# Last gate, third and fourth chunk: low parts by an accumulating DMA instead of VectorE's subtraction

## The chip, the cores and the metric

The kernel runs on one core of one Trainium2 chip. What counts is the device time of one execution in microseconds; a run's number is the median of several executions. The kernel before the change takes 1843.85 us (three runs, 1843.67 to 1844.14).

The engines are called by their names in the profile: PE (TensorE matmuls), PEld (TensorE's weight loads, which overlap the matmuls), DVE (VectorE), ACT (ScalarE), POOL (GpSimd) and SP (SyncE, which issues nearly all DMAs). L118 is line 118 of the kernel; a line can be a helper's.

## What is computed

The reference is a decoder of two layers on 512 tokens of width 2048, in float32. Layer 0 mixes by sparse attention, layer 1 by stick-breaking attention. After its mixer each layer does the same:

```
x = layer_norm(ALPHA * x + h, ln_g[i], ln_b[i])
x = x + (p[i] @ w_ple[i]) * sigmoid(x @ w_ple_gate[i])
```

The change is in the last product of the program, `x @ w_ple_gate[1]`: a 512 x 2048 array times a 2048 x 2048 matrix, followed by a sigmoid, a product and a sum. It is called the last gate here.

## The kernel before

Activations are held transposed: sixteen blocks of 128 features by 512 tokens. A product is a loop over the sixteen blocks of 128 weight rows, the k-blocks, which adds into PSUM banks of 128 output features by 512 tokens.

**Three matmuls for one.** TensorE takes its operands in a shorter form (fp32r). To keep float32 accuracy each operand is split: the high part is the number rounded to that form, the low part is what is left, number minus high part. `mm3` (L144 to L147) issues three matmuls for each product of two such pairs: high with high (L145), high weights with low activations (L146), low weights with high activations (L147). So the low weights `wl` are first needed by the third matmul of a k-block.

**How a weight block gets there.** SP loads raw weights, two k-blocks in one DMA, into one of three `raw` buffers (`next_raw`, L225). `plain_items` takes each k-block of it through `split` (L140): ScalarE copies `raw` into `wh` (which rounds it), and VectorE subtracts `wh` from `raw` into `wl`. Both come from rings of three buffers (`weight_parts`). A profile row shows L118 for every operation that ScalarE and VectorE issue, because a recording helper issues them there; the tiles' names tell them apart.

**The order of the work.** TensorE's order is the order of the program text. ScalarE, VectorE, SP and GpSimd get theirs from a scheduler that simulates the program when it is built, apart from the pieces that are pinned. Within an engine the instructions then run strictly in that order. `Ahead` is an iterator over weight blocks: it holds `n` blocks that are written down in the program ahead of the matmuls that use them, two by default, and so says how far ahead the text of the program asks for a block. How far ahead it can really be made is set by the buffers.

**The last gate.** Its 2048 output features are done in chunks of 512, 512, 512, 256, 128 and 128 (`LAST_PARTS`). The first two run interleaved, in eight banks. The third and the fourth run one after the other, each over sixteen k-blocks, with four banks and with two: twelve and six matmuls for a k-block. While a chunk runs, the pieces of the chunk before are put between its matmuls: `gated` (ScalarE's sigmoid out of the bank into `sg`, VectorE's product with `E` and its sum onto `f`) and `store` (a DMA from SP to the output, L1311). The two chunks of 128 have their weights loaded eight k-blocks to a DMA (L206) and copied four k-blocks at a time.

Of the kernel before, what the change touches and what calls it, by code (L numbers as in the profile page):

```python
# [11 lines left out]
F32R = mybir.dt.float32r  # L12
I32 = mybir.dt.int32
AF = mybir.ActivationFunctionType
ALU = mybir.AluOpType
# [6 lines left out]
NK = D // 128  # L22
# [24 lines left out]
def run(gen):  # L47
    for _ in gen:
        pass


def steps(gen, n):
    for _ in range(n):
        next(gen, None)
# [23 lines left out]
def trunk_kernel(  # L78
# [16 lines left out]
    nc = tc.nc  # L95
# [31 lines left out]
    act, dve, pool = (Paced(e) for e in (nc.scalar, nc.vector, nc.gpsimd))  # L127
# [9 lines left out]
    def bank(i, name="ps"):  # L137
        return psum.tile([128, 512], F32, name=name, tag=f"bank{i}")

    def split(hi, lo, src, eng=dve):  # L140
        act.activation(hi, src, AF.Copy)
        eng.tensor_tensor(lo, src, hi.bitcast(F32), ALU.subtract)
# [16 lines left out]
    def fblock(n):  # L159
        return F[n // 4][:, n % 4]  # L160
# [12 lines left out]
    units = []  # L173
# [10 lines left out]
    raws = deque()  # L184
    halves = []
    sent = [0]
# [5 lines left out]
    def next_raw():  # L192
        while sent[0] < len(units) and len(raws) < (6 if homes and sent[0] in kv_units else 3):
            housed[0] += 1
            if homes and sent[0] in kv_units and housed[0] % 2:
                raw = homes[housed[0] // 2 % 3]
            else:
                raw = top.tile([128, 2, 512], F32, name="raw", tag="raw", bufs=3)
            unit = units[sent[0]]
            if len(unit) == 1:  # L200
                _, k, n = unit[0].shape
            else:
                k, n = 2, unit[-1]
            raw = raw.rearrange("p a n -> p (a n)")[:, : k * n].rearrange("p (k n) -> p k n", k=k)
            if len(unit) == 1:
                nc.sync.dma_start(raw, unit[0])  # L206
            else:
                src, a, b, c0, n = unit
                rows = src.rearrange("(k p) n -> p k n", p=128)
                step = b - a  # L210
                if sent[0] < 2:

                    for i, cut in enumerate(((0, H if sent[0] else NSEL, T), (0, T))):
                        for lo, hi in zip(cut, cut[1:]):
                            halves.append((raw[:, i, lo:hi], rows[:, a + i * step, c0 + lo : c0 + hi]))
                    if len(halves) == 6:
                        for n in (1, 3, 4, 2, 5, 0):
                            nc.sync.dma_start(*halves[n])
                elif isinstance(c0, tuple):

                    for half, out in enumerate(raw.rearrange("p k (h n) -> h p k n", h=2)):
                        at = D // 2 * half + c0[0]
                        nc.sync.dma_start(out, rows[:, a : b + 1 : step, at : at + n // 2])
                else:
                    nc.sync.dma_start(raw, rows[:, a : b + 1 : step, c0 : c0 + n])  # L225
            raws.append(raw)
            sent[0] += 1
        return raws.popleft()
# [41 lines left out]
    def weight_parts():  # L270
        return tuple(top.tile([128, 512], F32R, name=n, tag=n, bufs=3) for n in ("wh", "wl"))

    def plain_items(jobs):
        for n, nk in jobs:
            if n <= 128:
                for k in range(0, nk, 4):
                    if k % 8 == 0:
                        raw = next_raw()
                    parts = weight_parts()
                    four = [w[:, : 4 * n].rearrange("p (k n) -> p k n", k=4) for w in parts]  # L280
                    split(*four, raw[:, k % 8 : k % 8 + 4])
                    yield from zip(*([w[:, a] for a in range(4)] for w in four))
                continue
            for _ in range(nk // 2):
                raw = next_raw()
                for a in range(2):
                    wh, wl = weight_parts()
                    split(wh[:, :n], wl[:, :n], raw[:, a])
                    yield wh, wl
# [36 lines left out]

    def plain_stream(*jobs):
        return Ahead(plain_items(jobs), 2)

    def gemm_w(items, get, banks, n=512, order=range(NK)):  # L330

        for i, kb in enumerate(order):
            wh, wl = next(items)
            x = get(kb)
            for j, out in enumerate(banks):
                a, b = j * 128, min(n, (j + 1) * 128)
                mm3(out[: b - a], (wh[:, a:b], wl[:, a:b]), x, i == 0, i == len(order) - 1)
                yield
# [62 lines left out]
    def pumped(gen, every=1):  # L401

        for i, _ in enumerate(gen):
            if bg and i % every == 0:
                one()
            yield

    def drain():
        while bg:
            one()  # L410
# [290 lines left out]
    for k in (4, 5, 6, None, 7, None, 0, 1, 2, 3):  # L701
        if k is None:
            first = 4 * (units[-1][1] == 14)
# [338 lines left out]
    def finish_layer(layer, resid, last, keep, early, ahead):  # L1042
# [112 lines left out]
        for c in SEVENS:  # L1155
            M = product_banks(3 - c)
            gemm = pumped(gemm_s(wo, four, M), 9 if c == 1 else 7)
            if c == 2:
                steps(gemm, 35)
                parts = weight_parts()  # L1160
# [49 lines left out]
        raw = next_raw()  # L1210
# [44 lines left out]
        fourth = embed(3, (2, 3, 4, 5))  # L1255
        steps(fourth, 4)
        parts = LAST_PARTS if layer else PARTS
        gitems = plain_stream(*[(n, NK) for n in parts]).prime()

        def scaled(n):  # L1260
            dve.tensor_tensor(fblock(n), fblock(n), rs, ALU.mult)
# [31 lines left out]
        with tc.tile_pool(name=f"pe{layer}", bufs=1, side="right") as ep:  # L1293

            places = deque((S, rs))
            if not layer:
                kv_room.append([[ep.tile([128, T], F32R, name=f"e{x}{n}") for x in "hl"] for n in range(2)])

            def gated(n, b, t=slice(0, T)):
                if layer:  # L1300
                    sg = ep.tile([128, T], F32, name="sg", tag="sg", bufs=4)[:, t]
                else:
                    places.rotate(1)
                    sg = places[0]
                act.activation(sg, b[:, t], AF.Sigmoid)
                dve.tensor_tensor(sg, sg, E[n][:, t], ALU.mult)
                dve.tensor_tensor(fblock(n)[:, t], fblock(n)[:, t], sg, ALU.add)

            def store(n, k, t=slice(0, T)):
                rows = last[n * 128 : (n + k) * 128, t].rearrange("(j p) t -> p j t", p=128)  # L1310
                nc.sync.dma_start(rows, F[n // 4][:, n % 4 : n % 4 + k, t])  # L1311

            def close(n, b):
                for t in (slice(0, H), slice(H, T)):
                    gated(n, b, t)
                    store(n, 1, t)

            banks = two[0]
            plan = list(zip(parts[1:], ((2, 3, 4, 5), (6, 7, 0, 1), (4, 5), (2, 3)))) + [(0, ())]
            if layer:  # L1320
                plan[3:] = [(128, (0,)), (128, (1,)), (0, ())]
            for c, (n, where) in enumerate(plan):
                part = BLOCKS[layer][c]
                for j, b in enumerate(banks):
                    if len(banks) == 1:
                        bg.append(lambda n=part[j], b=b: close(n, b))
                        continue
                    bg.append(lambda n=part[j], b=b: gated(n, b))
                    if j % 2 and part[j - 1] + 1 == part[j]:
                        bg.append(lambda n=part[j - 1]: store(n, 2))  # L1330
                    elif j % 2:
                        bg.extend(lambda n=n: store(n, 1) for n in part)
                bg.extend(early.get(c, ()))
                if not n:
                    break
                if c:
                    banks = [bank(b, "g") for b in where]
                    order = range(NK) if layer or c < 3 else PAIRS
                    gemm = gemm_close(gitems, banks[0]) if where == (1,) else gemm_w(gitems, plain, banks, n, order)
                else:  # L1340
                    banks = two[1]
                gemm = pumped(gemm, 4 if n == 512 else 2)
                if c == 3:
                    steps(gemm, 14 if layer else 6)
                    ahead(gemm)
                run(gemm)
                drain()
            drain()
# [41 lines left out]

    pk_, pv_ = ExitStack(), ExitStack()
    finish_layer(0, xT, x2, (pk_, pv_), first_sums, first_blocks)


# [174 lines left out]
    class Sticks:  # L1569
# [3 lines left out]
        units = [(3, 3), (1, 1), (3, 2), (1, 0), (3, 1), (2, 2), (3, 0), (2, 1), (0, 0), (2, 0)]  # L1573
# [211 lines left out]
    with ExitStack() as keep:  # L1785
        finish_layer(1, x2, outT, (keep, keep), lambda E8: {}, lambda gemm: None)
# [53 lines left out]
```

## Time and profile before

| | |
|---|---|
| median of three runs | 1843.85 us |
| the profiled execution, its span | 1842.2 us |
| PE busy | 1835.4 us, 9568 matmuls |
| VectorE busy in the whole run | 1377.9 us |
| ScalarE busy in the whole run | 989.8 us |
| GpSimd busy in the whole run | 4.7 us, 20 instructions |
| third chunk of the last gate | 1750.1 to 1793.6 us |
| fourth chunk | 1793.6 to 1815.4 us |
| last matmul starts | 1837.09 us |

The profile gives the profiled execution's span, from its first to its last instruction, and no other time for it; the difference to the median of the runs is 1.65 us. Its page has busy times per engine, the chain of work that ended last, and groups of equal instructions; the views used here beside the page are the waits of an engine, the windows (busy time of each engine in a stretch), the timeline of single instructions, and the groups in a stretch by form. In a group's row the number before the bar is the count; behind it stand the busy time in us, the mean duration in ns, and the engine's idle time before these instructions with what ended it. A matmul's row in the timeline shows 0.39 us, while the next starts 0.23 us later: they are pipelined.

### The profile page before, as it was taken

Reading aid. Unit: us, or ns where it says so; the run is one execution under the profiler, and the core shown is the slowest. Engines: PE = TensorE matmul, PEld = TensorE weight load, DVE = VectorE, ACT = ScalarE, POOL = GpSimd, SP = SyncE. Lnnn points to the kernel's source line nnn. Section 1 sums busy time; section 2 is a strip of 40 time slices with the busy share of each in tenths; the row PEclk is TensorE's granted clock in tenths of the full one; section 3 lists DMA queues with packets and bytes.
Section 4 is the critical chain, followed back from the end, with each engine's and each line's share of the span. In section 5 each row is a group of like instructions: output and inputs, shape, how many; then the busy total and the mean of one; then the engine's idle time right before and its main releaser. Section 6 shows DMA issues by size and latency. Waiting matters only on the chain.

```text
span 1842.2 us, 26158 instructions
## 1 busy us (share of the span) xinstructions
PE 1835.4 (100%) x9568; PEld 1580.4 (86%) x9568; DVE 1377.9 (75%) x2721; ACT 989.8 (54%) x1801; POOL 4.7 (0%) x20
## 2 busy tenths in 40 slices
PE   9999999999999999999999999999999999999998
PEld 8898888888888899888888899998888889988887
DVE  5668678575556789976568998888878789987434
ACT  3546333455555544575346544468888754557322
POOL 0000000000000000000000000000000000000000
PEclk9999999999999999999999999999999999999999
DMA  6442333322222344333437633323122245343333
GB/s 199 125 121 69 92 94 101 92 69 69 69 59 69 107 123 114 125 116 103 138 110 236 198 101 100 104 91 92 58 69 80 66 118 149 109 123 101 115 102 115
DMA packets 118000, 197.68 MB, mean 107 GB/s; under 512 B 9200, under 2 KB 37872, under 8 KB 117872
## 3 DMA queue, kind: packets, MB, share of 16 engines
q1 hardware_dynamic: 117872, 196.02, 35.9%
q8 instruction: 75, 1.23, 0.3%
q14 instruction: 53, 0.43, 0.1%
HBM read 187.60 MB, written 8.39 MB: 106 GB/s over the span
## 4 chain that ended last, share of the span: by engine, by line
PE 99%; DMA 0%; DVE 0%; ACT 0%; SPq 0%; issue 0%; ACTq 0%
PE g L145 13%; PE g L147 13%; PE g L146 13%; PE m L147 7%; PE m L145 7%; PE m L146 7%; PE o L146 4%; PE o L145 4%; PE o L147 4%; PE q L146 3%; PE q L147 3%; PE q L145 3%; PE iq L147 1%; PE iq L146 1%; PE iq L145 1%; PE z L1639 1%
## 5 line engine op out<-in xcount | busy, mean ns | idle before, releaser
L118 ACT ACTIVATE wh<-raw 128x512 fp32r<-128x512 f32 (+2 forms) x597 | 336.7, 565 | 537.9 <-PE g L146 211.2
L118 DVE TENSOR_TENSOR wl<-raw,wh 128x512 fp32r<-128x512 f32 (+2 forms) x596 | 361.5, 607 | 272.1 <-ACT wh L118 256.6
L145 PE MATMUL g<-xh,wh 128*128 128x512 f32 x1023 | 403.1, 394 | 0.0
L147 PE MATMUL g<-xh,wl 128*128 128x512 f32 x1023 | 399.0, 390 | 0.0
L146 PE MATMUL g<-xl,wh 128*128 128x512 f32 x1023 | 398.9, 390 | 0.0
L147 PEld LDWEIGHTS g<-xh,wl 128*128 128x128 f32 x1023 | 192.0, 188 | 40.7
L146 PEld LDWEIGHTS g<-xl,wh 128*128 128x128 f32 x1023 | 192.3, 188 | 37.2
L145 PEld LDWEIGHTS g<-xh,wh 128*128 128x128 f32 x1023 | 192.2, 188 | 37.1
L146 PE MATMUL o<-xl,wh 128*128 128x512 f32 x256 | 99.7, 390 | 0.0
L145 PE MATMUL o<-xh,wh 128*128 128x512 f32 x256 | 99.6, 389 | 0.0
L147 PE MATMUL o<-xh,wl 128*128 128x512 f32 x256 | 99.6, 389 | 0.0
L145 PE MATMUL q<-xh,wh 128*128 128x512 f32 x256 | 99.6, 389 | 0.0
L146 PE MATMUL q<-xl,wh 128*128 128x512 f32 x256 | 99.6, 389 | 0.0
L147 PE MATMUL q<-xh,wl 128*128 128x512 f32 x256 | 99.6, 389 | 0.0
L147 PE MATMUL m<-c,sl 128*128 128x256 f32 x320 | 90.9, 284 | 0.0
L145 PE MATMUL m<-c,sh 128*128 128x256 f32 x320 | 90.7, 283 | 0.0
L146 PE MATMUL m<-c,sh 128*128 128x256 f32 x320 | 90.5, 283 | 0.0
L118 ACT ACTIVATE sh<-f 128x512 fp32r<-128x512 f32 x77 | 48.0, 624 | 67.6 <-DVE f L118 64.8
L147 PE MATMUL m<-xh,wl 128*128 128x256 f32 x256 | 72.6, 284 | 0.0
L145 PE MATMUL m<-xh,wh 128*128 128x256 f32 x256 | 72.5, 283 | 0.0
L146 PE MATMUL m<-xl,wh 128*128 128x256 f32 x256 | 72.4, 283 | 0.0
L118 ACT ACTIVATE sh<-st 128x512 fp32r<-128x512 f32 x70 | 43.6, 624 | 52.2 <-DVE st L118 51.5
(378 smaller groups left out, 4061.0 us busy)
## 6 DMA issues: line engine op xcount, KB each, us to landing
raw<-w_in_a SPq DMA_DIRECT2D x95, 512.0 KB, 3.7
raw<-w_in_b SPq DMA_DIRECT2D x64, 512.0 KB, 3.7
raw<-w_ple_gate SPq DMA_DIRECT2D x44, 512.0 KB, 3.9
raw<-w_o_a SPq DMA_DIRECT2D x24, 512.0 KB, 4.5
raw<-w_o_b SPq DMA_DIRECT2D x24, 512.0 KB, 4.5
f<-w_kv_b SPq DMA_DIRECT2D x16, 512.0 KB, 4.6
raw<-w_kv_b SPq DMA_DIRECT2D x16, 512.0 KB, 4.3
raw<-w_ple_gate SPq DMA_DIRECT2D x24, 256.0 KB, 2.9
```

Of the source, the lines that this page charges most:

```text
L118: ins = method(*args, **kw)
L145: pe.matmul(out, a[0], b[0], start=start, stop=False)
L146: pe.matmul(out, a[0], b[1], start=False, stop=False)
L147: pe.matmul(out, a[1], b[0], start=False, stop=stop)
L1639: pe.matmul(z, down if kb % 2 else tri, p, start=False, stop=n == 1, skip_group_check=True)
```

## The change

In the last gate of layer 1, for the third chunk (512 features) and the fourth (256), the low part is no longer made by VectorE. For each of the 32 k-blocks

- ScalarE copies `raw` with the factor -1 into `wm`, which leaves the negated high part there;
- GpSimd issues a DMA (L341 of the changed kernel) that reads the same raw weights from HBM once more and adds them onto `wm`, which leaves raw minus high part, the low part;
- ScalarE copies `raw` into `wn`, the high part, as before into `wh`.

`wn` and `wm` are new rings of six buffers each, in a pool that exists during the last gate only. While these 32 blocks are asked for, `Ahead` is set to hold five blocks instead of two. `first` is the index of the weights' place in the list of loads.

```
+    def summed_items(pool_, parts):
+        first = sent[0] - len(raws)
+        for n in parts:
+            for _ in range(NK // 2):
+                src, a, b, c0, n = units[first]
+                first += 1
+                raw = next_raw()
+                for i, row in enumerate((a, b)):
+                    wh = pool_[0].tile([128, 512], F32R, name="wn", tag="wn", bufs=6)[:, :n]
+                    wl = pool_[0].tile([128, 512], F32R, name="wm", tag="wm", bufs=6)[:, :n]
+                    act.activation(wl, raw[:, i], AF.Copy, scale=-1.0)
+                    nc.gpsimd.dma_start(wl, src[row * 128 : row * 128 + 128, c0 : c0 + n], accum_op=ALU.add)
+                    act.activation(wh, raw[:, i], AF.Copy)
+                    yield wh, wl
...
-        gitems = plain_stream(*[(n, NK) for n in parts]).prime()
+        tail_pool = []
+
+        def tail_items():
+            jobs = [(n, NK) for n in parts]
+            yield from plain_items(jobs[:2])
+            gitems.n = 5
+            yield from summed_items(tail_pool, parts[2:4])
+            gitems.n = 2
+            yield from plain_items(jobs[4:])
+
+        gitems = Ahead(tail_items(), 2) if layer else plain_stream(*[(n, NK) for n in parts])
+        gitems.prime()
...
         with tc.tile_pool(name=f"pe{layer}", bufs=1, side="right") as ep:
...
+            tail_pool.append(ep)
```

TensorE's order does not move; only the names of its weight tiles change. GpSimd's program, which ended with the masks of layer 1's attention, gets the DMAs as its last work. Before:

```order
20 L1563 AFFINE_SELECT wk<-wk 128x128
21 L1567 AFFINE_SELECT gone_12011<-gone_12011 128x128
22 L1567 AFFINE_SELECT gone_12012<-gone_12012 128x128
23 L1836 UNCONDITIONAL_BRANCH
24 L1836 ISA
```

and now:

```order
20 L1590 AFFINE_SELECT wk<-wk 128x128
21 L1594 AFFINE_SELECT gone_12011<-gone_12011 128x128
22 L1594 AFFINE_SELECT gone_12012<-gone_12012 128x128
23 L341 DMA wm<-w_ple_gate 128x512 x16
24 L341 DMA wm<-w_ple_gate 128x256 x16
25 L1863 UNCONDITIONAL_BRANCH
26 L1863 ISA
```

All 32 DMAs stand there in the order of the blocks, with nothing between them.

On ScalarE, at the end of the fourth chunk (`wh` 128x512 are the copies for the two closing chunks, `sg` the sigmoids of the fourth), the order before was

```order
1373 L118 ACTIVATE sg<-g 128x512
1374 L118 ACTIVATE wh<-raw 128x256 x9
1375 L118 ACTIVATE wh<-raw 128x512 x2
1376 L118 ACTIVATE sg<-g 128x512
1377 L118 ACTIVATE wh<-raw 128x512
```

and is now

```order
1425 L118 ACTIVATE wn<-raw 128x256
1426 L118 ACTIVATE wm<-raw 128x256
1427 L118 ACTIVATE wn<-raw 128x256
1428 L118 ACTIVATE wm<-raw 128x256
1429 L118 ACTIVATE wh<-raw 128x512 x2
1430 L118 ACTIVATE wn<-raw 128x256
1431 L118 ACTIVATE wm<-raw 128x256
1432 L118 ACTIVATE wh<-raw 128x512
1433 L118 ACTIVATE sg<-g 128x512 x2
```

Each block has two copies there in place of one, the one into `wn` first, and two copies for the fifth chunk have moved ahead of the last block's pair. On VectorE the 32 subtractions are gone, and the products and sums of `gated` stand without them in between.

## The prediction

> **What bounds the kernel now.** I read the page's busy shares and chain first, then TensorE's waits over the whole run, and then the windows of the three stretches that the change can reach.
>
> ```profile
> PE 1835.4 (100%) x9568; PEld 1580.4 (86%) x9568; DVE 1377.9 (75%) x2721; ACT 989.8 (54%) x1801; POOL 4.7 (0%) x20
> ...
> PE 99%; DMA 0%; DVE 0%; ACT 0%; SPq 0%; issue 0%; ACTq 0%
> ...
> PE spun L167 <- DVE xl L118: 1.4, 1, 1.4
> PE z L145 <- DVE t L116: 0.3, 1, 0.3
> ```
>
> TensorE (PE) is the bound from end to end: 99% of the chain is its matmuls, and in the whole run it waited for another engine twice, 1.7 us together, both far from the last gate. The subtractions that the change removes are never what TensorE waits for. The windows below are the third chunk, the fourth chunk, and the two closing chunks; columns are length, busy time of PE, PEld, DVE, ACT and POOL, granted clock, share of the DMA engines and GB/s.
>
> ```profile
> 1750.10:1793.60 43.50, 43.50 (x193) 36.02 (x193) 15.72 (x24) 11.62 (x20) 0.00 (x0) 1.00 0.33 106
> 1793.60:1815.40 21.80, 21.80 (x97) 18.04 (x97) 12.16 (x24) 9.53 (x21) 0.00 (x0) 1.00 0.56 172
> 1815.40:1837.30 21.90, 21.90 (x100) 18.12 (x98) 8.16 (x14) 4.85 (x10) 0.00 (x0) 1.00 0.19 62
> 975.00:985.00 10.00, 10.00 (x46) 8.28 (x45) 6.69 (x14) 6.12 (x13) 0.00 (x0) 1.00 0.87 271
> ```
>
> PE is busy for all of each stretch, at a granted clock of 1.00, while VectorE (DVE) is busy 15.72 of 43.50 us and 12.16 of 21.80 us. So a lighter VectorE has nothing to give here: the best case is no change, and the question is whether the new supply line keeps pace.
>
> **The pace that the supply must keep.** TensorE takes one block of 128 weight rows (wh and wl) after the other. A row of the timeline has start, length, engine, line, operation and tiles.
>
> ```profile
> 1744.67 0.63 ACT L118 ACTIVATE wh<-raw 128x512 fp32r<-128x512 f32 x1 [2.09 <-PE g L146]
> ...
> 1747.39 0.63 ACT L118 ACTIVATE wh<-raw 128x512 fp32r<-128x512 f32 x1 [2.09 <-PE g L146]
> ...
> 1790.48 0.39 PE L146 MATMUL g<-xl,wh 128*128 128x512 f32 x1
> ...
> 1790.71 0.39 PE L147 MATMUL g<-xh,wl 128*128 128x512 f32 x1
> ...
> 1790.91 0.42 ACT L118 ACTIVATE wh<-raw 128x256 fp32r<-128x256 f32 x1 [2.30 <-PE g L146]
> 1790.94 0.39 PE L145 MATMUL g<-xh,wh 128*128 128x512 f32 x1
> ...
> 1791.17 0.19 PEld L147 LDWEIGHTS g<-xh,wl 128*128 128x128 f32 x1
> ...
> 1793.63 0.42 ACT L118 ACTIVATE wh<-raw 128x256 fp32r<-128x256 f32 x1 [2.30 <-PE g L146]
> ...
> 1793.95 0.58 ACT L118 ACTIVATE sg<-g 128x512 f32<-128x512 f32 x1
> ...
> 1803.15 0.42 ACT L118 ACTIVATE wh<-raw 128x256 fp32r<-128x256 f32 x1 [0.94 <-PE g L146]
> ...
> 1804.51 0.42 ACT L118 ACTIVATE wh<-raw 128x256 fp32r<-128x256 f32 x1 [0.94 <-PE g L146]
> ```
>
> ScalarE (ACT) refills a buffer whenever TensorE frees one, so its steps show TensorE's: 1747.39 - 1744.67 = 2.72 us for a block in the third chunk, 1804.51 - 1803.15 = 1.36 us in the fourth. 16 blocks each make 43.5 and 21.8 us, the windows above.
>
> In the change, wm (the new wl) has six buffers. Block k may be written when TensorE has done with block k-6, and is needed when block k's first L147 loads its weights. From that come two allowances for "GpSimd's time for one DMA, S, plus its landing after that, Ld". In the fourth chunk: ScalarE starts 0.04 us after the releasing matmul ends (1790.48 + 0.39 to 1790.91), writes wn, 0.32 us later (1793.63 to 1793.95) wm for 0.42 us, so wm stands about 0.8 us after the block's end. It is needed five blocks and 0.25 us later (1790.94 to 1791.17): 5 x 1.36 + 0.25 - 0.8 = 6.25 us. In the third chunk, with 0.63 us instead of 0.42, it is 5 x 2.72 + 0.25 - 1.15 = 12.7 us. These are allowances for delay; for rate, S must stay under 2.72 and 1.36 us.
>
> **The change part by part.** Removed: 32 subtractions on VectorE, 16 of each width.
>
> ```profile
> L118 DVE TENSOR_TENSOR wl<-raw,wh 128x512 fp32r<-128x512 f32 x16 | 11.1, 693 | 24.9 <-ACT wh L118 24.2 <-PE g L146 0.7
> L118 ACT ACTIVATE wh<-raw 128x512 fp32r<-128x512 f32 x17 | 10.7, 632 | 29.0 <-PE g L146 28.2 <-DVE wl L118 0.7
> L118 DVE TENSOR_TENSOR wl<-raw,wh 128x256 fp32r<-128x256 f32 x16 | 6.8, 424 | 13.5 <-ACT wh L118 13.5
> L118 ACT ACTIVATE wh<-raw 128x256 fp32r<-128x256 f32 x16 | 6.7, 418 | 17.0 <-PE g L146 17.0
> ```
>
> That is 11.1 + 6.8 = 17.9 us of VectorE, all of it under matmuls: worth 0. A gain is excluded because PE had no wait there.
>
> Added on ScalarE: 32 negated copies, priced as the plain copies of those rows, 16 x 0.632 + 16 x 0.418 = 16.8 us. ScalarE goes to about 11.6 + 10.1 = 21.7 of 43.5 us and 9.5 + 6.7 = 16.2 of 21.8 us: it fits, cost 0.
>
> Added on GpSimd: 32 DMAs, which read the weights a second time: 16 x 256 KB and 16 x 128 KB, or 4.2 and 2.1 MB, some 96 GB/s in either chunk. No DMA of GpSimd and none that accumulates is in the trace, so S and Ld are bounded by SP's plain ones (KB each, median us from issue to landing; then the duration of the issue in ns).
>
> ```profile
> raw<-w_ple_gate SPq DMA_DIRECT2D x44, 512.0 KB, 3.9
> ...
> raw<-w_ple_gate SPq DMA_DIRECT2D x24, 256.0 KB, 2.9
> ...
> raw<-w_ple_gate SPq DMA_DIRECT2D x32, 128.0 KB, 2.5
> ...
> L225 SPq DMA_DIRECT2D raw<-w_ple_gate x13: 367/368/368, 1748.8 to 1804.1; - x13
> ```
>
> S from below: SP's issue, 0.37 us. S from above: one DMA at a time, the whole landing, 2.5 us for 128 KB and 2.9 for 256 KB. Ld from below 2.5 us; from above twice that, 5.0, because the sum reads two operands.
>
> In the third chunk both ends pass: S is at most 2.9 against 2.72, short by 0.2 us over the ten blocks that the six buffers don't cover, 2 us against an allowance of 12.7. In the fourth chunk eleven DMAs (blocks 5 to 15) have to be issued after it has begun; the first can start at 0.8 us, the last must have landed at 15 x 1.36 + 0.25 = 20.65 us. Where S is over 1.36, TensorE is therefore late by 0.8 + 11 S + Ld - 20.65 = **11 S + Ld - 19.85 us**. Lower ends: below nothing, so 0. Upper ends: 11 x 2.5 + 5.0 - 19.85 = 12.7 us. I take the lower end, since SP's issue is the nearest row (the same two-dimensional DMA from the same tensor) and the formula stays at nothing up to S = 1.58 us at Ld = 2.5, over four times that row.
>
> The page "DMA: Bandwidth & Descriptors" of the Trainium skill (section on the anatomy of one DMA on the gpsimd path) states about 2.0 us plus bytes over 436e3 for such a DMA; an estimate by it is 2.3 us for 128 KB, inside the 6.25 us, and no run here shows it.
>
> DMA traffic: the fourth chunk goes from 172 to some 268 GB/s, and with the second operand more engine time than that; 271 GB/s at a share of 0.87 were reached before (the last window row above) without a PE wait. 0, with Ld's upper end standing for crowding.
>
> Moved: two copies for the fifth chunk now stand on ScalarE ahead of block 15's pair. Their raw load starts when block 11 has been copied, at 6 x 1.36 + 0.8 = 9.0 us, and lands at 12.9 (3.9, row above); wm 14 stands at 13.0, the two copies end near 14.2, and wm 15 near 15.0. That leaves 5.65 us of the allowance for S + Ld, and 2.9 are used at my value. SP has no other wait added; GpSimd has nothing else queued.
>
> After the last gate nothing changes:
>
> ```profile
> 1837.09 0.28 PE L366 MATMUL g<-xh,wl 128*128 128x256 f32 x1
> 1837.41 0.66 ACT L118 ACTIVATE sg<-g 128x256 f32<-128x256 f32 x2 [7.78 <-PE g L366]
> ```
>
> **Sum.** The profiled execution spans 1842.2 us, 1.65 below the median of the runs, 1843.85, which covers what lies around the span. Removed 0, ScalarE 0, DMAs 0, moved 0; I add 0.3 for a partly exceeded allowance: 1844.2 us.
>
> **Rivals.** First, and on the slower side: GpSimd's own time per DMA sets the rate. Place: L341's 128x256 DMAs in the fourth chunk. It decides from S = 1.58 us, and over the 3.7 us that make 0.2% from S = 1.91. For it: a path that this kernel never used, and a second operand to describe. Against it: the 0.37 us row. At S = 2.5, Ld = 2.5: 27.5 + 2.5 - 19.85 = 10.2 us, so 1854.0; at S = 1.91 1847.6.
>
> Second: the sums land late, S + Ld over 6.25 us, with the DMA engines crowded. Every round of six buffers then pays the excess; at 10 us two rounds, 2 x 3.75 = 7.5 us, 1851.4. Against it: the slowest row above needs 3.9 us at 512 KB.
>
> Third: VectorE holds GpSimd off while it works. In the fourth chunk it still has 4 pairs for the third chunk's gates:
>
> ```profile
> L118 DVE TENSOR_TENSOR f<-f,sg x8: 683/692/693, 1752.1 to 1801.3; 128x512 f32<-128x512 f32 x8
> ...
> L118 DVE TENSOR_TENSOR sg<-sg,e x4: 683/690/695, 1794.6 to 1800.3; 128x512 f32<-128x512 f32 x4
> ```
>
> If each shut GpSimd out for its 0.69 us, 8 x 0.69 = 5.5 us are lost; at S = 1.36 that makes 0.8 + 15.0 + 5.5 + 2.5 - 20.65 = 3.1 us, 1847.0. The page "SBUF — State Buffer" of the Trainium skill (section "SBUF: two separate sides") warns of such a trap, VectorE keeping GpSimd from writing descriptors during a two-port operation. By its section "Who interferes with whom" tensor_tensor has no such mode and contends only with GpSimd's reads, which speaks for a small chance; this trace can't show either.
>
> Fourth: faster, 1843.0 or below. It would need PE to lose the 0.23 us step between matmuls, for which no row speaks.
>
> **How the numbers follow.** Forecast, no wait or one under 3.7 us: 0.55, at 1844.2, own range 1843.4 to 1847.5. GpSimd's rate 0.28, late landing 0.11, VectorE's hold 0.03 (it stays within 0.2%), faster 0.03. A measurement of this kernel can't tell less than about 0.2%, 3.7 us, from no change. So faster 0.03, same 0.55 + 0.03 = 0.58, slower 0.28 + 0.11 = 0.39. The range runs from 1843.0 to 1858, the upper ends of S and Ld (12.7 us) and 1.5 us more; what lies above is S over 2.5.
>
> **What would show it.** Right: PE's waits name neither wm nor DMA in the last 92 us, the fourth chunk stays at 21.8 us, and GpSimd's DMAs stand at under 1.4 us each. Wrong: PE L147 waits for wm in the fourth chunk. If the waits grow from block to block and GpSimd's DMAs follow each other without a gap, it is the first rival; if GpSimd has gaps and issue to landing is over 6 us, the second; if its DMAs are long only beside VectorE's pairs, the third. A wait already in the third chunk would mean S over 2.72 us, above my bound.

## The result and the profile after

The changed kernel takes 1853.83 us (1852.69 to 1855.94), the kernel before 1843.85: a ratio of 1.0056, 95% interval 1.0038 to 1.0074. It is slower by 10 us, or 0.56%, and the interval lies clear of 1. In a later comparison it took 1852.70 us (1850.68 to 1854.73) against 1843.63, a ratio of 1.0050 (1.0037 to 1.0063). The profiled execution of it spans 1854.2 us, 1.74 us less than its own time of 1855.94; before spanned 1842.2. So the traces have 12.0 us to explain.

First the page of the changed kernel (busy times, the queue that GpSimd feeds, the chain), then TensorE's waits over the whole run.

```profile
PE 1841.1 (99%) x9568; PEld 1583.6 (85%) x9568; DVE 1360.9 (73%) x2689; ACT 1002.3 (54%) x1833; POOL 32.4 (2%) x52
...
q0 software_dynamic: 4608, 6.29, 2.1%
...
PE 94%; issue 3%; POOL 1%; DMA 1%; ACT 0%; DVE 0%; SPq 0%; POOLq 0%; ACTq 0%
```

```profile
PE g L147 <- DMA wm<-w_ple_gate: 4.3, 3, 3.8
PE g L145 <- ACT wh L118: 2.1, 1, 2.1
```

VectorE lost its 32 subtractions (17.0 us of busy time), ScalarE gained 32 copies (12.5 us), GpSimd 32 DMAs. TensorE, which waited nowhere in the last gate before, now has one long wait for a sum (`wm`), two short ones, and one long wait for an ordinary copy (`wh`), which the change did not touch. But the waits make only 6.4 of the 12.0 us. The rest is in TensorE's own timeline, here at the end of the second chunk and at the end of the fourth:

```profile
1746.80 0.39 PE L147 MATMUL g<-xh,wl 128*128 128x512 f32 x1
1749.32 0.50 PE L145 MATMUL g<-xh,wh 128*128 128x512 f32 x1 [2.13 <-ACT wh L118]
...
1752.07 0.63 PE L147 MATMUL g<-xh,wl 128*128 128x512 f32 x1
1752.50 0.63 PE L145 MATMUL g<-xh,wh 128*128 128x512 f32 x1
...
1753.78 0.63 PE L145 MATMUL g<-xh,wn 128*128 128x512 f32 x1
...
1819.62 0.39 PE L146 MATMUL g<-xl,wn 128*128 128x512 f32 x1
1823.80 0.79 PE L147 MATMUL g<-xh,wm 128*128 128x512 f32 x1 [3.79 <-DMA wm<-w_ple_gate]
1824.39 0.63 PE L145 MATMUL g<-xh,wn 128*128 128x512 f32 x1
...
1829.08 0.55 PE L147 MATMUL g<-xh,wl 128*128 128x512 f32 x1
```

Behind each hole the matmuls start 0.43 us apart for a while (from 1751.22 to 1754.21, and eleven steps from 1824.39 to 1829.08) instead of 0.227. The windows of the same execution (columns as in the prediction) show it as a granted clock of 0.83 and 0.68:

```profile
1740.00:1750.00 10.00, 7.87 (x34) 5.93 (x32) 3.87 (x6) 4.19 (x9) 1.73 (x2) 1.00 0.82 215
1750.00:1760.00 10.00, 10.00 (x38) 8.03 (x38) 2.77 (x4) 3.92 (x8) 2.59 (x3) 0.83 0.95 236
1760.00:1797.60 37.60, 37.60 (x168) 31.14 (x167) 2.77 (x4) 14.51 (x30) 12.08 (x14) 1.00 0.80 179
1797.60:1820.00 22.40, 21.88 (x93) 16.85 (x91) 7.41 (x11) 11.58 (x29) 9.52 (x11) 1.00 0.87 199
1820.00:1827.00 7.00, 3.21 (x9) 2.53 (x9) 1.71 (x3) 1.19 (x2) 0.00 (x0) 0.68 0.59 151
```

In the order of time, counted from one matmul's start to the next, less the usual step: the hole before 1749.32 costs 1749.32 - 1746.80 - 0.23 = 2.3 us; the slow matmuls behind it 2.0 (15 steps in 5.40 us instead of 3.40); the hole before 1823.80 costs 1823.80 - 1819.62 - 0.23 = 3.95; the slow ones behind it 2.7 (13 steps in 5.66 instead of 2.95). That is 10.95 us. Two short waits for sums in the fourth chunk and the stretched steps around these and around one more block (between 1808.70 and 1814.61) make 1.3; counted as waits alone they are only 0.5 (4.3 - 3.8). Together this is 12.25 us for the 12.0 of the spans, so nothing large is left over.

What came late? ScalarE and GpSimd around the two holes:

```profile
1746.56 0.63 ACT L118 ACTIVATE wm<-raw 128x512 fp32r<-128x512 f32 x1 [5.81 <-DMA raw<-w_ple_gate]
...
1748.65 0.61 ACT L118 ACTIVATE wh<-raw 128x512 fp32r<-128x512 f32 x1
...
1810.52 0.40 ACT L118 ACTIVATE wm<-raw 128x256 fp32r<-128x256 f32 x1
1816.04 1.15 ACT L118 ACTIVATE wh<-raw 128x512 fp32r<-128x512 f32 x2 [5.12 <-DMA raw<-w_ple_gate]
...
1817.40 0.40 ACT L118 ACTIVATE wm<-raw 128x256 fp32r<-128x256 f32 x1
```

```profile
1811.21 0.86 POOL L341 DMA_DIRECT2D wm<-w_ple_gate  x1 [0.82 <-ACT wm L118]
1818.10 0.86 POOL L341 DMA_DIRECT2D wm<-w_ple_gate  x1 [6.02 <-ACT wm L118]
```

Both times ScalarE stands still for more than 5 us because a raw load has not landed, while work that TensorE needs sooner stands behind the waiting copy. At 1746.56 that is the last `wh` of the second chunk, behind four copies for the third. At 1816.04 it is the pair of block 15, behind the two `wh` copies for the fifth chunk; its sum is issued at 1818.10, and TensorE has it at 1823.80.

And the loads are late. SP's raw loads near the first hole, before and after (count, duration of the issue in ns, first and last start; then the time from issue to landing):

```profile
L225 SPq DMA_DIRECT2D raw<-w_ple_gate x2: 368/368/368, 1737.9 to 1743.3; - x2
...
DMA to landing us min/median/max: 3.9/4.1/4.4
```

```profile
L225 SPq DMA_DIRECT2D raw<-w_ple_gate x2: 367/368/368, 1738.8 to 1740.0; - x2
...
DMA to landing us min/median/max: 7.8/7.8/7.9
```

The four 512 KB loads of the closing chunks took 3.8 to 3.9 us before, and now 4.5 to 9.5; the longest is the one issued at 1806.5, for which ScalarE waits until 1816.04:

```profile
L206 SPq DMA_DIRECT2D raw<-w_ple_gate x4: 368/368/534, 1806.5 to 1818.3; - x4
...
DMA to landing us min/median/max: 4.5/7.5/9.5
```

### The profile page after: what moved, and what is told of

Its sections match the earlier page's. It is cut to its first block, busy times and chain, and to the rows that moved or that the text cites. A ratio compares the mean times of both kernels' runs of the same rounds, so it can differ in the third digit from the quotient of the medians.

```text
span 1854.2 us, 26209 instructions
## 1 busy us (share of the span) xinstructions
PE 1841.1 (99%) x9568; PEld 1583.6 (85%) x9568; DVE 1360.9 (73%) x2689; ACT 1002.3 (54%) x1833; POOL 32.4 (2%) x52
## 3 DMA queue, kind: packets, MB, share of 16 engines
q0 software_dynamic: 4608, 6.29, 2.1%
## 4 chain that ended last, share of the span: by engine, by line
PE 94%; issue 3%; POOL 1%; DMA 1%; ACT 0%; DVE 0%; SPq 0%; POOLq 0%; ACTq 0%
PE g L145 11%; PE g L147 11%; PE g L146 11%; PE m L147 7%; PE m L145 7%; PE m L146 7%; PE o L146 4%; PE o L147 4%; PE o L145 4%; PE q L145 3%; PE q L146 3%; PE q L147 3%; POOL wm L341 1%; PE iq L147 1%; PE iq L145 1%
## 5 line engine op out<-in xcount | busy, mean ns | idle before, releaser
L118 ACT ACTIVATE wh<-raw 128x512 fp32r<-128x512 f32 (+3 forms) x565 | 319.8, 567 | 489.5 <-PE g L146 158.0
L118 DVE TENSOR_TENSOR wl<-raw,wh 128x512 fp32r<-128x512 f32 (+3 forms) x564 | 343.5, 610 | 251.5 <-ACT wh L118 238.5
L145 PE MATMUL g<-xh,wh 128*128 128x512 f32 x927 | 367.0, 396 | 2.1 <-ACT wh L118 2.1
L147 PE MATMUL g<-xh,wl 128*128 128x512 f32 x927 | 363.1, 392 | 0.0
L146 PE MATMUL g<-xl,wh 128*128 128x512 f32 x927 | 362.8, 391 | 0.0
L147 PEld LDWEIGHTS g<-xh,wl 128*128 128x128 f32 x927 | 174.7, 188 | 37.7 <-DVE wl L118 0.4
L145 PEld LDWEIGHTS g<-xh,wh 128*128 128x128 f32 x927 | 175.0, 189 | 36.1 <-ACT wh L118 2.6
L146 PEld LDWEIGHTS g<-xl,wh 128*128 128x128 f32 x927 | 175.0, 189 | 33.7
```

Of the source, the lines that this page charges most:

```text
L118: ins = method(*args, **kw)
L145: pe.matmul(out, a[0], b[0], start=start, stop=False)
L146: pe.matmul(out, a[0], b[1], start=False, stop=False)
L147: pe.matmul(out, a[1], b[0], start=False, stop=stop)
```

## The experiments

Three theories. **A**: the added DMA work makes the raw loads late, and ScalarE's fixed order hands the delay on to TensorE. **B**: the new order (copies five blocks ahead, six buffers) does it without the traffic. **C**: the sums themselves land too late for their blocks. Each comparison ran beside the kernel before, which took 1843.54 to 1843.63 us in the median.

**The order without the DMAs.** Rings, text order and five blocks ahead as in the change, but VectorE subtracts again:

```
-                    act.activation(wl, raw[:, i], AF.Copy, scale=-1.0)
-                    nc.gpsimd.dma_start(wl, src[...], accum_op=ALU.add)
-                    act.activation(wh, raw[:, i], AF.Copy)
+                    split(wh, wl, raw[:, i])
```

> The accumulating DMAs are taken out and VectorE subtracts again, but the rings of six, the five blocks ahead and with them ScalarE's order (the third chunk's copies ahead of the second chunk's last ones, two copies for the fifth chunk ahead of block 15's) stay. Theory A (the added DMA work makes the raw loads late, and ScalarE's fixed order hands that on to TensorE): no load is late, TensorE waits for nothing in the last gate, 1843.9 us within 0.5. Theory B (the order alone blocks ScalarE, whatever the DMAs do): both waits stay, at least half of the 10 us, 1849 us or more.

Measured 1843.67 us, ratio 1.0001 (0.9992 to 1.0011). TensorE waits nowhere in the last gate, although ScalarE still waits for raw loads, with copies for the third chunk ahead of the second chunk's last `wh` and with the two copies for the fifth chunk ahead of block 15's, as in the change. The third chunk's window shows DMA engines at a share of 0.22:

```profile
ACT wn L118 <- DMA raw<-w_ple_gate: 4.5, 2, 2.3
```

```profile
1760.00:1793.60 33.60, 33.60 (x150) 27.85 (x149) 9.02 (x16) 7.14 (x14) 0.00 (x0) 1.00 0.22 72
```

B falls: the order alone costs nothing. (This run has one copy on ScalarE for each block, the change has two; the next one keeps both.)

**The DMAs without the addition.** The second operand is left out; `wm` then gets the raw weights themselves:

```
-                    nc.gpsimd.dma_start(wl, src[...], accum_op=ALU.add)
+                    nc.gpsimd.dma_start(wl, src[...])
```

> The DMAs stay on GpSimd and read the same weights, but overwrite wm and don't add (the low part is then the whole weight, so the output is another). It takes the second operand out and leaves the issue and the second read from HBM. Theory A with the second operand as the price: the DMA engines' share between 1760 and 1797 us falls from 0.80 towards 0.55, the raw loads of 512 KB land in under 6 us, and the time falls below 1849 us. Theory A with the second read as the price: share and waits stay, 1853 us. Theory C (the sum itself lands too late for its block): wm lands about 2 us sooner, and only the wait for wm shrinks.

Measured 1845.60 us, ratio 1.0010 (1.0001 to 1.0020). So the second copy on ScalarE and the second reading of the bytes cost 2 us together, and the addition the other 7 to 8. The share between 1760 and 1793.6 us is 0.59, as expected; that the 512 KB loads would land in under 6 us holds only for the two near the first place (5.8 to 6.0), while later ones still took up to 9.2. Its waits, GpSimd's time for a DMA (min, median, max in ns), and the queue's share:

```profile
PE g L147 <- DMA wm<-w_ple_gate: 1.5, 1, 1.5
```

```profile
L341 POOL DMA_DIRECT2D wm<-w_ple_gate x32: 527/527/670, 1737.4 to 1812.2; - x32
```

```profile
q0 software_dynamic: 4608, 6.29, 1.3%
```

The packets of the same 6.29 MB take 2.1% of the DMA engines' time with the addition and 1.3% without, 1.6 times as much. (Packets of an engine can overlap in this measure, since shares above 1 occur, so it is time in the engines and not a pure rate.) The Trainium skill ("Collectives: The Full Stack", Part 3 on the bandwidth ceiling) says of a ReduceScatter that the add halves its rate because it reads two sources. The ratio here is 1.6, on the same side.

**One chunk at a time.** Only the third chunk summed, then only the fourth:

```
-            yield from summed_items(tail_pool, parts[2:4])
+            yield from summed_items(tail_pool, parts[2:3])
...
-            yield from plain_items(jobs[4:])
+            yield from plain_items(jobs[3:])
```

> Only the third chunk gets its low parts by DMA; the fourth is as before. Theory A: the wait at the end of the second chunk and the slow matmuls behind it stay, about 4 us; the wait for block 15's wm in the fourth chunk goes, and with it about 8 us: 1847 to 1849 us. Theory C: most of the loss is the fourth chunk's short blocks, so 1844.5.

Measured 1848.48 us (1845.12 to 1850.41), ratio 1.0026 (1.0015 to 1.0037). Only the first hole is there, in this profile without a slow stretch behind it:

```profile
PE g L145 <- ACT wh L118: 1.8, 1, 1.8
```

The fourth alone (`jobs[:3]` plain, `parts[3:4]` summed):

> Only the fourth chunk gets its low parts by DMA. Theory A: no wait at the end of the second chunk; the wait for block 15's wm stays, about 8 us with the slow matmuls behind it, unless the loads ahead of it are sooner: 1848 to 1852 us. Together with the run on the third chunk alone the two losses should make up the 10 us. Theory C: the same or more, 1850 to 1853.

Measured 1850.47 us, ratio 1.0039 (1.0024 to 1.0054). Only the second hole is there:

```profile
PE g L147 <- DMA wm<-w_ple_gate: 3.6, 1, 3.6
```

The losses, 4.9 and 6.9 us, make 11.8 together, against 9 to 10 for both at once. Within the intervals, of some 2 to 3 us on either side of each, that adds up: two separate holes. A sum that is late for its own block (C) would show in the middle of the chunks; what is there makes 1.3 us in the changed kernel.

**Half of the sums.** Of each raw load only the first block is summed by DMA, the second is subtracted by VectorE:

```
+                    if i:
+                        split(wh, wl, raw[:, i])
+                    else:
```

> In each pair of blocks that one raw load brings, only the first gets its low part by the accumulating DMA; the second is subtracted by VectorE as before the change. Rings, order of the text and five blocks ahead stay. If the load on the DMA engines is the cause, it halves: the engines' share in the third chunk should come out near 0.55 (0.22 with VectorE alone, 0.80 with all sums), as high as with plain reads (0.59), and the loss near theirs: 1844 to 1847 us. If each accumulating DMA costs its own block something, half of the loss stays: about 1849 us. If GpSimd's rate were the cause, nothing is left, since its DMAs come only every second block: 1843.9 us, but then the raw loads would still be 9 us late.

Measured 1845.26 us, ratio 1.0008 (0.9999 to 1.0018), with the DMA engines at 0.54 in the third chunk:

```profile
1760.00:1793.60 33.60, 33.60 (x149) 27.81 (x149) 6.30 (x10) 10.29 (x21) 5.96 (x7) 1.00 0.54 134
```

Half of the sums cost 1.7 us, not 5: the loss is no price for each DMA. What decides is when the copy that waits for a load lets go. At the first place the four profiles line up (us from the start; the first column is when the first raw load has landed and ScalarE goes on):

| run | ScalarE goes on | last `wh` of the second chunk starts | TensorE waits for it |
|---|---|---|---|
| VectorE subtracts | 1742.50 | 1744.86 | 0 |
| plain reads | 1744.47 | 1746.57 | 0.2 |
| half of the sums | 1745.54 | 1747.12 | 0.5 |
| the change | 1746.56 | 1748.65 | 2.1 |

A last `wh` that starts by about 1746.5 is nearly in time; what is later than that, TensorE pays almost in full. (With half of the sums three copies stand ahead of it, in the other runs four.)

**The load kept, the order changed.** Now the other half of theory A. The whole change with all its DMAs, but the copies of the fourth and the closing chunks are pinned to the order of the text, in which block 15's pair stands ahead of the two `wh` copies (and in each pair `wm` ahead of `wn`):

```
+        def held(made):
+            while True:
+                was, pinned[0] = pinned[0], True
+                it = next(made, None)
+                pinned[0] = was
+                if it is None:
+                    return
+                yield it
...
-            yield from summed_items(tail_pool, parts[2:4])
+            yield from summed_items(tail_pool, parts[2:3])
+            yield from held(summed_items(tail_pool, parts[3:4]))
...
-            yield from plain_items(jobs[4:])
+            yield from held(plain_items(jobs[4:]))
```

> The whole change, but the copies of the fourth chunk and of the closing chunks are kept in the order of the program text, which puts both copies of block 15 ahead of the two wh 128x512 copies for the fifth chunk. The work and the traffic are the same. If the order on ScalarE hands the late 512 KB load on to TensorE, the wait of 3.8 us for wm near 1820 and the slow stretch behind it go, and what is left is the third chunk's loss: 1846 to 1849 us, with a wait of TensorE for wh near 1749 of about 2 us. If the last sum itself lands too late for its block, the wait for wm stays: 1852 to 1854 us. A new wait is possible where the closing chunk needs its wh, which then come later.

Measured 1848.10 us (1846.99 to 1850.58), ratio 1.0028 (1.0017 to 1.0039). The second hole is gone (the 0.6 us are some blocks earlier, at 1816.81), although the closing loads still take up to 9.6 us; the first stays:

```profile
PE g L145 <- ACT wh L118: 2.0, 1, 2.0
...
PE g L147 <- DMA wm<-w_ple_gate: 0.6, 1, 0.6
```

With the third chunk pinned too (`held(summed_items(tail_pool, parts[2:4]))`):

> As e_pin4, and the third chunk's copies are kept in program order too, so that the second chunk's last wh copies no longer stand behind wm copies whose raw loads are late. By the theory of late loads and fixed order, the wait for wh near 1749 goes; but the first wm copies then start some 5 us later, and their sums (5.6 us and more from issue to landing) come late for the first blocks of the third chunk: a wait of TensorE L147 for wm of 1 to 5 us at 1750 to 1757 in its place, and a total of 1845 to 1850 us. If the order alone were the cause, the total is that of before, 1843.9 us.

Measured 1845.31 us, ratio 1.0010 (1.0000 to 1.0019). Both holes are gone: the second chunk's last `wh` starts at 1741.51, ahead of the first `wm`. The wait for `wm` that was expected in their place, 1 to 5 us at 1750 to 1757, did not come; two waits of 0.5 us together stand in the fourth chunk. And this with DMA engines as crowded as ever and raw loads behind 1746 that land later than in the change, where those took 7.8 to 10.5 us (its wait, one of the two places, a window, its raw loads):

```profile
PE g L147 <- DMA wm<-w_ple_gate: 0.5, 2, 0.3
```

```profile
1802.96 0.39 PE L146 MATMUL g<-xl,wn 128*128 128x512 f32 x1
1803.68 0.50 PE L147 MATMUL g<-xh,wm 128*128 128x512 f32 x1 [0.33 <-DMA wm<-w_ple_gate]
```

```profile
1750.00:1760.00 10.00, 10.00 (x46) 8.29 (x45) 3.05 (x5) 5.18 (x10) 3.46 (x4) 1.00 1.11 256
```

```profile
L225 SPq DMA_DIRECT2D raw<-w_ple_gate x3: 368/368/410, 1746.3 to 1756.9; - x3
...
DMA to landing us min/median/max: 10.5/10.6/11.8
```

Counted from one start to the next, the late and stretched steps between 1802.96 and 1808.99 make 1.4 us. They explain most of this run's 1.7 us, and they are theory C in small: sums that land late for their own blocks. So neither the load alone (this run, 1.7 us) nor the order alone (the first run, nothing) makes the loss; it takes both. At the first place the pinned order also moves the first sum from 1737.5 to 1743.0, so the crowding begins later there; at the second place the traffic was the same.

**Is the slow spacing the hole's doing?** 16 matmuls into a free bank, results unused, ahead of block 15 of the fourth chunk, where TensorE stood idle:

```
+                if layer and c == 2:
+                    steps(gemm, 30)
+                    warm = bank(2, "warm")
+                    for _ in range(16):
+                        pe.matmul(warm, neg, XH[0], start=True, stop=True)
```

> The whole change, with 16 more matmuls into a free bank (of the tiles neg and XH[0], results unused) ahead of block 15 of the fourth chunk, 16 x 0.227 = 3.6 us, in the place where TensorE waited 3.95 us. If the wait alone costs, the time stays at 1853.8 us: the dummies fill the hole and nothing else. If TensorE is slowed by the idle stretch itself, the spacing of the matmuls behind it stays at 0.227 us instead of 0.43, and the 2.5 us of that stretch are saved: 1851.0 to 1851.6 us. If the slow spacing has another cause (weights late, crowding), it stays as it was at 1853.8. The first wait near 1749 is untouched.

Measured 1852.18 us (1850.81 to 1853.26). Behind the filled hole the matmuls stand 0.23 us apart, though the sum still comes late (the wait of 0.69 us, behind 3.6 us of dummies):

```profile
1818.57 3.79 PE L1377 MATMUL warm<-xh,neg 128*128 128x512 f32 x16
...
1823.50 0.50 PE L147 MATMUL g<-xh,wm 128*128 128x512 f32 x1 [0.69 <-DMA wm<-w_ple_gate]
1823.84 0.39 PE L145 MATMUL g<-xh,wn 128*128 128x512 f32 x1
```

The time is 0.6 us above the 1851.0 to 1851.6 that were expected if the slow stretch goes, and it does not by itself separate this run from the changed kernel. So the next run fills both holes, beside the changed kernel itself:

```
+                if tail_mark and (c, kb) == (1, NK - 1):
+                    warm = bank(6, "warm")
+                    for _ in range(10):
+                        pe.matmul(warm, neg, XH[0], start=True, stop=True)
```

> The changed kernel itself, beside the next one on the same chip, for a comparison closer than two separate medians: 1853 to 1854 us by every theory.

> As e_warm, with 10 more dummy matmuls (10 x 0.227 = 2.3 us) ahead of the last block of the second chunk, where TensorE waited 2.3 us for wh: both waits are filled, and neither shortens. If an idle stretch costs only itself, the time is that of the changed kernel, 1853.8 us. If TensorE runs slower behind it, both slow stretches go (2.0 + 2.5 us), and the matmuls behind 1749 and behind 1824 stand 0.227 us apart: 1849 to 1850.5 us.

Measured 1851.03 us (1850.43 to 1851.70) against the changed kernel's 1852.70 (1850.68 to 1854.73, where 1853 to 1854 was expected). The ranges overlap, so the medians alone prove nothing. But both slow stretches are gone from its profile:

```profile
1747.05 2.43 PE L368 MATMUL warm<-xh,neg 128*128 128x512 f32 x10
1749.32 0.39 PE L145 MATMUL g<-xh,wh 128*128 128x512 f32 x1
...
1817.05 3.79 PE L1385 MATMUL warm<-xh,neg 128*128 128x512 f32 x16
...
1821.52 0.50 PE L147 MATMUL g<-xh,wm 128*128 128x512 f32 x1 [0.23 <-DMA wm<-w_ple_gate]
1821.86 0.40 PE L145 MATMUL g<-xh,wn 128*128 128x512 f32 x1
```

Its span is 1849.3 us, 4.9 below that of the changed kernel's first profile, where the slow stretches make 2.0 + 2.7. Its median is lower by only 1.7, and lies 0.5 us above what was expected, most likely because the slow stretch does not follow every hole. In the profile with only the third chunk summed, the hole of 1.8 us was followed by matmuls 0.23 us apart. The mean granted clock that each execution shows goes the same way. With only the third chunk summed, the two executions at 1.000 took 1845.12 and 1846.59 us, the five at 0.998 and 0.999 took 1848.27 to 1850.41. The eight of the changed kernel took 1850.68 to 1852.70 us at 0.999, 1852.06 to 1854.73 at 0.998, and 1854.66 and 1855.94 at 0.997; the five with both holes filled stand at 0.999 and 1.000. So the slow stretches are worth 4.7 us in the execution that was profiled first, and by an estimate from these medians some 2 us in the typical one; they go with much of the spread.

## Why the prediction was right or wrong

The likeliest case, no change at 1844.2 us, did not come, and the result lies above that case's own range of 1843.4 to 1847.5. The wide range of 1843.0 to 1858 does hold 1853.83, but by luck: its upper end was added up from GpSimd's rate and the landing of one DMA, and not from SP's late loads and the slow matmuls behind the holes.

- **What bounds the kernel, and the removed work.** Right. TensorE is the bound, and VectorE's 17 us bought nothing.
- **Added on ScalarE, at 0.** Right as far as capacity goes: 14.51 us busy of 37.60 and 11.58 of 22.40 in the chunks, and 12.5 us more in the whole run where 16.8 were priced. What it cost was not time but place in the order.
- **GpSimd's time for a DMA, S.** Taken at the lower end of 0.37 to 2.5 us, near SP's issue. It is 0.862 us, more than twice that row, and under the 1.36 us of a block:

```profile
L341 POOL DMA_DIRECT2D wm<-w_ple_gate x32: 862/862/1013, 1737.5 to 1818.1; - x32
...
DMA to landing us min/median/max: 3.1/5.6/9.8
```

- **The first rival, GpSimd's rate, at 1854.0 us**, has the number of the result but not its cause; that they agree is chance. The formula 11 S + Ld - 19.85 at 0.862 and 5.6 us is -4.8, so nothing. In the fourth chunk GpSimd stands idle about 0.5 us or more ahead of its DMAs, but for two that follow another directly (the rows at 1811.21 and 1818.10 show 0.82 and 6.02 us).
- **Landing, Ld.** Bounded by 2.5 and 5.0 us and used at the lower end. The median is 5.6 us, above the upper end, and the longest 9.8. S + Ld is then 5.6 to 6.5 us (by whether landing counts from the start or the end of GpSimd's instruction), where the allowance was 6.25. In the middle of the fourth chunk that cost 1.3 us.
- **DMA traffic, at 0: the step that failed.** The argument was that 271 GB/s at a share of 0.87 had been reached before without a wait. The rate in the crowded stretches is no higher (179 to 236 GB/s), but the share is 0.80 to 0.95, for 16 blocks on end and with 512 KB loads among them. A moved byte of the sums stays in the engines longer than a plain one: in the window 1806 to 1818 of the changed kernel the two queues take nearly the same share, and GpSimd's moves half the megabytes. Without the addition its queue took 23.6% for 0.66 MB in that window, beside 58.4% for 1.95.

```profile
q0 software_dynamic: 1043, 0.94, 52.4%
q1 hardware_dynamic: 2624, 1.84, 51.6%
```

 The prediction looked at what the new DMAs would suffer from it, and not at what SP's loads would: 3.9 us became 7.8 to 9.5.
- **Moved, at 0: the same step, one link further on.** The mechanism was right, step by step: the two copies for the fifth chunk stand ahead of block 15's pair and wait for their raw load. Its sizes were off. The load started 8.9 us after the chunk's start at 1797.6, as forecast (9.0), but took 9.5 us instead of 3.9, so that the last `wm` stood at 20.2 us instead of 15.0. S + Ld, put at 2.9, took 5.7 (1818.10 to 1823.80), as much as the whole 5.65 that were left without the delay. An estimate shows what the late load alone did: block 14's sum was issued at 1811.21, so block 15's would have followed one block later, near 1812.6, and landed 5.6 us after that, near 1818.2, in time for 1819.85. The price was 3.95 us for the hole and up to 2.7 behind it. Pinning the order took this hole away.
- **A place that was not looked at.** The same thing happens at the end of the second chunk, a stage that the change seems not to touch: with five blocks asked for ahead, copies for the third chunk stand ahead of the second chunk's last `wh`. The prediction looked at the order of ScalarE at the end of the fourth chunk only. This was worth 2.3 us for the hole and 2.0 behind it in the profile, 4.9 us in the run with the third chunk alone.
- **The second rival** (sums late, DMA engines crowded, 1851.4 us at a chance of 0.11) is nearest to what happened. Its sign, GpSimd with gaps and landing near 6 us, came; its price did not: not each round of six buffers pays, only two places do, and there through SP's loads. **The third** (VectorE holding GpSimd off) did not show: minimum and median of GpSimd's DMAs are both 862 ns, the longest 1013, beside VectorE's work or not.
- **The price of a hole.** Each wait was to be paid once. The matmuls behind it ran at about half their pace for 3 to 5 us.

Left open: why an accumulating DMA stays longer in the engines, and what decides whether a hole of about 2 us is followed by a slow stretch. No version tried beats the kernel before, as TensorE had no wait there to lose.

## What to carry to other kernels

When work moves onto the DMA engines, ask first what it does to the loads that are there already: a load that lands in twice its time is nearly harmless by itself (1.7 us here with the loads late and the copies in order) and costs when an in-order engine has more urgent work queued behind the copy that waits for it. So look at the order on every engine wherever the prefetch depth changes, at the start of the changed stage as well as at its end, and put the copies in the order in which they are needed. In this case a byte that the DMA adds counted for about 1.6 plain ones, and a hole of 2.3 us in TensorE's work cost up to 2.0 more behind it.

## What was not expected of the hardware

- **The clock behind a hole.** After 2.1 and 3.8 us without a matmul, TensorE's matmuls started 0.43 us apart for 3 to 5 us, then 0.227 again; filling the holes with unused matmuls kept them at 0.23. After a hole of 1.8 us, with only the third chunk summed, the slow stretch was absent in the profile; the granted clocks suggest that it came in five of the seven executions. "TensorE: Matmul & The Clock Gate" of the Trainium skill (Part 1, on the HAM clock gate) describes this: half the clock after an idle window of about 3.4 us that runs freely, and full clock again after about as long under work. The spacing agrees, 0.427 us against 0.227, nearly half the pace, and so does its start, at once behind the second hole and 1.9 us behind the end of the first; holes of 2.1 us are shorter than the window that it names, and they sufficed here.
- **GpSimd's time for a DMA** of 128 rows: 862 ns with the addition, 527 without, against 368 for SP's, and the same for 128 and for 256 KB.
- **An accumulating DMA** took 1.6 times the packet time per byte of the same DMA without the addition (2.1% against 1.3% for 6.29 MB). That this is not only the crowding is shown by the run with half of the sums: 1.1% for 3.15 MB, 1.7 times as much per byte, at a DMA share of 0.54. The two 512 KB loads near the first place landed after 3.9 to 4.4 us before, 5.8 to 6.0 beside plain reads and 7.8 to 7.9 beside the sums.
